# Two-head stores in 16 KB runs, and transposes on VectorE instead of TensorE, in a batched x·yᵀ kernel

## The chip, the cores and the metric

The kernel runs on one core of a Trainium2 chip. The time is the device time of one execution in microseconds. Ten runs of the kernel before have a median of 307.43 us (307.35 to 307.79).

## The reference

```python
batch, n_heads, seq_t, seq_s, channels = 8, 12, 512, 512, 64
def reference(x, y):        # x: [8, 12, 512, 64], y: [8, 12, 512, 64], float32
    return np.einsum('bhtc,bhsc->bhts', x, y).astype(np.float32)
```

There are 96 heads (batch and head together). Each multiplies a 512 x 64 matrix by the transpose of another one and gives a 512 x 512 matrix of float32. The inputs are 25.2 MB, the output is 100.7 MB. The contraction runs over 64 channels, which lie innermost in memory, while TensorE contracts over partitions: so channels must be brought onto partitions first.

## The kernel before

The heads are taken in 12 groups (`NG`) of 8. Within a group they stand as two sets `a` of four heads (`G = 4`). A head takes 32 partitions (`Q`), and a partition holds 16 consecutive rows (`R`) of it.

`load(g)` (L52) issues two DMAs of 1 MB from the SP queue, y and then x. In each, a partition receives two runs of 4 KB, one per set. Three groups are loaded ahead (`AHEAD`, the depth of `lpool`).

`prepare(g)` (L65) is a generator; each `yield` is a step that the main loop takes at a place of its choice. The first step casts y and x to bf16 on GpSimd (L73, four casts of 128 x 1024 elements) and issues the load for three groups later. Two steps transpose y: eight 128 x 128 transposes on TensorE against an identity matrix (L82) fill a PSUM tile `pt`, which is copied out by VectorE (L88) or ScalarE (L90). Two more do the same for x (L95, L100, L102). Channels are then on partitions, 64 for each of the two sets.

The main loop (L109) takes each group and each set `a`. An output tile `ot` has 128 partitions, each with 16 rows of 512 columns, 32 KB. For each pair of rows `k` it issues eight matmuls (L122): four heads, each with 32 columns of weights, into four 32-partition strips of `pm`, for two rows. ScalarE (L129) evicts even pairs from PSUM, VectorE (L131) odd ones. A step of the next group's `prepare` is taken at k = 0, 3 and 6 (L117). When the tile is full, one DMA of 4 MB stores it (L136): it is one contiguous piece of the output, a run of 32 KB per partition. The first and the last tile are stored in four pieces of 1 MB instead (L134).

All DMAs are issued on SP, in program order. A DMA that must wait holds back those behind it on SP. `ot` has three buffers: an eviction into a fourth tile waits until the first one's store has landed. Each engine takes its instructions in the order in which the scheduler of the framework wrote them.

Of the kernel before, what the change touches and what calls it, by code (L numbers as in the profile page):

```python
# [1 line left out]

# [5 lines left out]


@with_exitstack  # L10
def kernel(
    ctx: ExitStack,
    tc: tile.TileContext,
    x: bass.AP,
    y: bass.AP,
    out: bass.AP,
):

    nc = tc.nc
    B, H, T, C = x.shape
    _, _, S, _ = y.shape
    P = 128
    G = 4
    Q = P // G
    R = T // Q
    NG = B * H // (2 * G)  # L30
    K = R // 2
    AHEAD = 3
    fp32 = mybir.dt.float32
    bf16 = mybir.dt.bfloat16
    COPY = mybir.ActivationFunctionType.Copy
    assert C * 2 == P and S == T and R == 16

    xv = x.rearrange("b h t c -> (b h t c)").rearrange("(g a p n) -> g p a n", a=2, p=P, n=R * C)
    yv = y.rearrange("b h t c -> (b h t c)").rearrange("(g a p n) -> g p a n", a=2, p=P, n=R * C)
    ov = out.rearrange("b h t s -> (b h t s)").rearrange("(g a p n) -> g a p n", a=2, p=P, n=R * S)  # L40

    const = ctx.enter_context(tc.tile_pool(name="const", bufs=1))
    lpool = ctx.enter_context(tc.tile_pool(name="lpool", bufs=AHEAD))
    bpool = ctx.enter_context(tc.tile_pool(name="bpool", bufs=2))
    tpool = ctx.enter_context(tc.tile_pool(name="tpool", bufs=2))
    opool = ctx.enter_context(tc.tile_pool(name="opool", bufs=3))
    ptpool = ctx.enter_context(tc.tile_pool(name="ptpsum", bufs=2, space=bass.MemoryType.PSUM))
    pmpool = ctx.enter_context(tc.tile_pool(name="pmpsum", bufs=3, space=bass.MemoryType.PSUM))

    loaded = {}  # L50

    def load(g):  # L52
        xs = lpool.tile([P, 2, R, C], fp32)
        ys = lpool.tile([P, 2, R, C], fp32)
        nc.sync.dma_start(ys.rearrange("p a r c -> p a (r c)"), yv[g])  # L55
        nc.sync.dma_start(xs.rearrange("p a r c -> p a (r c)"), xv[g])
        loaded[g] = (xs, ys)

    for g in range(AHEAD):
        load(g)  # L60

    ident = const.tile([P, P], bf16)
    make_identity(nc, ident)

    def prepare(g, made):  # L65

        xs, ys = loaded.pop(g)
        yb = bpool.tile([P, R, 2, C], bf16)
        xb = bpool.tile([P, R, 2, C], bf16)
        for s, b in ((ys, yb), (xs, xb)):  # L70
            for half in range(2):
                rows = slice(half * K, (half + 1) * K)
                nc.gpsimd.tensor_copy(b[:, rows], s[:, :, rows].rearrange("p a r c -> p r a c"))  # L73
        if g + AHEAD < NG:
            load(g + AHEAD)
        yield
        yT = tpool.tile([P, G * Q, R], bf16)
        xT = tpool.tile([P, R, P], bf16)
        for half in range(2):
            pt = ptpool.tile([P, K, P], bf16)  # L80
            for k in range(K):
                nc.tensor.transpose(  # L82
                    pt[:, k, :], yb[:, half * K + k].rearrange("p a c -> p (a c)"), ident
                )
            dst = yT[:, :, half * K:(half + 1) * K]
            src = pt.rearrange("p k n -> p n k")
            if half == 0:
                nc.vector.tensor_copy(dst, src)  # L88
            else:
                nc.scalar.activation(dst, src, COPY)  # L90
            yield
        for half in range(2):
            pt = ptpool.tile([P, K, P], bf16)
            for k in range(K):
                nc.tensor.transpose(  # L95
                    pt[:, k, :], xb[:, half * K + k].rearrange("p a c -> p (a c)"), ident
                )
            dst = xT[:, half * K:(half + 1) * K]
            if half == 0:
                nc.vector.tensor_copy(dst, pt)  # L100
            else:
                nc.scalar.activation(dst, pt, COPY)  # L102
            yield
        made[g] = (xT, yT.rearrange("p n k -> p (n k)"))

    made = {}
    for _ in prepare(0, made):
        pass
    for g in range(NG):  # L109
        xT, yT = made.pop(g)  # L110
        steps = prepare(g + 1, made) if g + 1 < NG else iter(())
        for a in range(2):
            ot = opool.tile([P, R, S], fp32)
            otf = ot.rearrange("p r s -> p (r s)")
            edge = (g == 0 and a == 0) or (g == NG - 1 and a == 1)
            for k in range(K):
                if k in (0, 3, 6):  # L117
                    next(steps, None)
                pm = pmpool.tile([P, 2, S], fp32)
                for two in range(2):  # L120
                    for h in range(G):
                        nc.tensor.matmul(  # L122
                            pm[h * Q:(h + 1) * Q, two, :],
                            xT[a * C:(a + 1) * C, 2 * k + two, h * Q:(h + 1) * Q],
                            yT[a * C:(a + 1) * C, h * S:(h + 1) * S],
                            start=True, stop=True,
                        )
                if k % 2 == 0:
                    nc.scalar.activation(ot[:, 2 * k:2 * k + 2, :], pm, COPY)  # L129
                else:  # L130
                    nc.vector.tensor_copy(ot[:, 2 * k:2 * k + 2, :], pm)  # L131
                if edge and k % 2 == 1:
                    i, j = (2 * k - 2) * S, (2 * k + 2) * S
                    nc.sync.dma_start(ov[g, a][:, i:j], otf[:, i:j])  # L134
            if not edge:
                nc.sync.dma_start(ov[g, a], otf)  # L136


# [1 line left out]
_INS = ['x', 'y']  # L140
_OUTS = [((8, 12, 512, 512), 'float32')]


# [23 lines left out]
```

## Time and profile before

| | |
|---|---|
| profiled execution | 307.43 us |
| its span, first to last instruction | 305.7 us |
| instructions | 4378, of which PE 1920 matmuls and 1920 weight loads |
| busy share: PE, VectorE, ScalarE, GpSimd | 67%, 45%, 39%, 16% |
| HBM read, written | 25.17 MB, 100.66 MB, 412 GB/s over the span |
| granted PE clock | full to about 70 us, then half |
| 4 MB stores | 22, median 27.8 us from issue to landing |
| loads of 1 MB | 24, median 21.0 us (y) and 23.1 us (x) |

An idle engine costs nothing unless something waits for it. In a line of the costliest groups one reads: line, engine, operation, output and input with shapes, how often; then busy time in all and the mean of one in ns; then how long the engine stood idle before these instructions, and what ended most of that. In a line of the waits: engine, line and tile that waited, what ended the wait, us in all, how often, the longest. In a queue's line: kind, packets, MB, and the share of sixteen DMA engines' span that they took. A packet is one contiguous run that one DMA engine moves.

### The profile page before, as it was taken

The page shows a single profiled execution, that of the slowest core. Times are in us where ns is not written, and L with a number is a line of the kernel's source. Part 1 is how long each engine was busy: PE and PEld are TensorE (multiplying, and loading weights), DVE is VectorE, ACT ScalarE, POOL GpSimd, SP SyncE. Part 2 cuts the span into 40 slices and gives each one's busy share as a digit, 9 for nine tenths or more (in the row PEclk, how much of TensorE's full clock was granted, in tenths as well). Part 3 has the DMA queues.
Part 4 walks back from the last instruction along what each step waited for, and adds up shares of the span by engine and source line. Part 5 has one row for each costly group of instructions (what it writes and reads, how often), then busy time and mean ns, then how long its engine had stood idle before and what let it go on. Part 6 is the DMA issues. An engine that isn't in the chain of part 4 may idle for free.

```text
span 305.7 us, 4378 instructions
## 1 busy us (share of the span) xinstructions
PE 205.3 (67%) x1920; PEld 91.8 (30%) x1920; DVE 138.7 (45%) x120; ACT 119.7 (39%) x121; POOL 49.3 (16%) x54
## 2 busy tenths in 40 slices
PE   1899999969919918926953990980796976575000
PEld 1443234525304403512511530350252432222000
DVE  0465655657417607605633741670654664446000
ACT  1445537544423606605523441560644463325000
POOL 3754024300500500320140050041000000000000
PEclk9999999975555555755655555586555555555555
DMA  7999999999999999999999999999999999999980
GB/s 281 412 409 420 453 418 406 466 422 388 442 455 389 443 442 404 443 425 440 434 422 429 428 432 421 418 447 425 437 431 429 422 446 431 420 433 440 404 365 33
DMA packets 10867, 126.11 MB, mean 413 GB/s; under 512 B 864, under 2 KB 864, under 8 KB 7008
## 3 DMA queue, kind: packets, MB, share of 16 engines
q1 hardware_dynamic: 10848, 125.83, 97.2%
q8 instruction: 15, 0.25, 0.3%
q14 instruction: 4, 0.03, 0.0%
HBM read 25.17 MB, written 100.66 MB: 412 GB/s over the span
## 4 chain that ended last, share of the span: by engine, by line
DMA 49%; PE 30%; DVE 5%; issue 4%; ACT 3%; POOL 1%; SPq 0%; ACTq 0%
DMA out_dram<-ot 47%; PE pm L122 24%; DVE ot L131 4%; PE pt L95 4%; ACT ot L129 3%; DMA xs<-in_x_dram 2%; PE pt L82 2%; POOL xb L73 1%; ACT xT L102 0%; DVE xT L100 0%; SPq L55 0%; ACTq L129 0%; SPq L136 0%
## 5 line engine op out<-in xcount | busy, mean ns | idle before, releaser
L122 PE MATMUL pm<-yT,xT 64*32 64x512 bf16 x1536 | 160.7, 593 | 65.9 <-ACT ot L129 63.9
L131 DVE COPY ot<-pm 128x1024 f32<-128x1024 f32 x96 | 117.1, 1224 | 122.9 <-DMA out_dram<-ot 62.9
L129 ACT ACTIVATE ot<-pm 128x1024 f32<-128x1024 f32 x96 | 96.0, 1023 | 115.6 <-DMA out_dram<-ot 71.3
L122 PEld LDWEIGHTS <-xT 64*32 64x32 bf16 x1536 | 53.5, 119 | 147.9 <-issue 136.5
L73 POOL CAST yb<-ys 128x1024 bf16<-128x1024 f32 x24 | 24.3, 1041 | 143.6 <-PE pm L122 66.4
L82 PE MATMUL pt<-ident,yb 128*128 128x128 bf16 x192 | 24.2, 298 | 8.4 <-POOL yb L73 6.8
L102 ACT ACTIVATE xT<-pt 128x1024 bf16<-128x1024 bf16 x12 | 12.3, 1023 | 37.0 <-PE pt L95 30.2
L95 PE MATMUL pt<-ident,xb 128*128 128x128 bf16 x192 | 25.8, 310 | 1.3 <-DVE xT L100 0.8
L73 POOL CAST xb<-xs 128x1024 bf16<-128x1024 f32 x24 | 24.3, 1042 | 13.7 <-issue 4.9
L95 PEld LDWEIGHTS <-xb 128*128 128x128 bf16 x192 | 19.4, 143 | 22.6 <-issue 20.0
L82 PEld LDWEIGHTS <-yb 128*128 128x128 bf16 x192 | 19.5, 138 | 17.6 <-issue 8.2
L88 DVE COPY yT<-pt 128x1024 bf16<-128x1024 bf16 x12 | 14.6, 1215 | 8.4 <-PE pt L82 8.4
L90 ACT ACTIVATE yT<-pt 128x1024 bf16<-128x1024 bf16 x12 | 12.2, 1019 | 8.2 <-PE pt L82 8.2
L100 DVE COPY xT<-pt 128x1024 bf16<-128x1024 bf16 x12 | 8.3, 690 | 12.2 <-PE pt L95 9.7
L90 ACT ACT_TABLE_LOAD x1 | 1.3, 1283 | 0.7 <-PEq L151 0.7
masks.py:199 POOL TENSOR_SCALAR_AFFINE_SELECT ident<-ident 128x128 bf16<-128x128 bf16 x1 | 0.3, 292 | 0.1
masks.py:197 POOL MEMSET ident<- 128x128 bf16 x1 | 0.2, 204 | 0.3 <-POOLq L151 0.3
L151 POOL MEMSET const-float32-0.0<- 128x1 f32 x1 | 0.1, 98 | 0.2 <-issue 0.2
L151 POOL MEMSET const-bfloat16-1.0<- 128x1 bf16 x1 | 0.1, 102 | 0.0
L151 POOL MEMSET const-uint8-127<- 128x1 uint8 x1 | 0.1, 102 | 0.0
L151 POOL MEMSET const-float32-1.0<- 128x1 f32 x1 | 0.1, 98 | 0.0
## 6 DMA issues: line engine op xcount, KB each, us to landing
out_dram<-ot SPq DMA_DIRECT2D x22, 4096.0 KB, 27.8
ys<-in_y_dram SPq DMA_DIRECT2D x12, 1024.0 KB, 21.0
xs<-in_x_dram SPq DMA_DIRECT2D x12, 1024.0 KB, 23.1
out_dram<-ot SPq DMA_DIRECT2D x8, 1024.0 KB, 19.2
```

What stands on the lines that cost most here:

```text
L73: nc.gpsimd.tensor_copy(b[:, rows], s[:, :, rows].rearrange("p a r c -> p r a c"))
L82: nc.tensor.transpose(pt[:, k, :], yb[:, half * K + k].rearrange("p a c -> p (a c)"), ident)
L88: nc.vector.tensor_copy(dst, src)
L90: nc.scalar.activation(dst, src, COPY)
L95: nc.tensor.transpose(pt[:, k, :], xb[:, half * K + k].rearrange("p a c -> p (a c)"), ident)
L100: nc.vector.tensor_copy(dst, pt)
L102: nc.scalar.activation(dst, pt, COPY)
L122: nc.tensor.matmul(pm[h * Q:(h + 1) * Q, two, :], xT[a * C:(a + 1) * C, 2 * k + two, h * Q:(h + 1) * Q], yT[a * C:(a + 1) * C, h * S:(h + ...
L129: nc.scalar.activation(ot[:, 2 * k:2 * k + 2, :], pm, COPY)
L131: nc.vector.tensor_copy(ot[:, 2 * k:2 * k + 2, :], pm)
L151: nc = _bacc.Bacc("TRN2", target_bir_lowering=False, num_devices=1)
```

## The change

Groups are still 8 heads, but a head now takes 16 partitions (`G = 8`, `Q = 16`) of 32 rows each. A load puts one run of 8 KB on each partition. The four heads of a half group lie on 64 partitions.

`casts` casts in 32- and 64-partition pieces that also move data: the lower and the upper 32 channels of a half group go to different partitions of the bf16 tiles. For x, a pair of heads (`u`) has its own 32 partitions, and writes only its own slots of `xb`; the other slots are zeroed once at the start and stay zero. There are two such tiles, one per half.

`transposes` uses VectorE's transpose of 32 x 32 blocks, from SBUF to SBUF, for x and for y. The identity matrix, the transposes on TensorE and their PSUM tiles are gone, and `pm` has four buffers.

A matmul contracts over 128 partitions, channels of two heads, and its weights are 128 columns: 64 rows of head u = 0 interleaved with 64 of u = 1. The zeros in `xb` keep the two heads apart. One matmul thus serves two heads.

An output tile has 128 partitions of 8 rows, 16 KB, of two heads; neighbouring partitions belong to heads that are 2 MB apart in the output. Each tile is 2 MB and is stored whole. `ot` has seven buffers. VectorE evicts one pair of rows in four, ScalarE three. The order of all instructions is the order in which the program writes them (`manual_schedule`). For the first group the casts are shared among VectorE, ScalarE and GpSimd; later ones are all on GpSimd.

```diff
-    G = 4
+    G = 8
-    K = R // 2
+    K = 8
+    E = R // K
+    D = 32
-    ov = out.rearrange("b h t s -> (b h t s)").rearrange("(g a p n) -> g a p n", a=2, p=P, n=R * S)
+    ov = out.rearrange("b h t s -> (b h t s)").rearrange(
+        "(o u h q n) -> o h q u n", u=2, h=2, q=Q * E, n=K * S
+    )
...
+    zeroed = [const.tile([P, K, E, 2, D], bf16, name=f"xb{half}") for half in range(2)]
...
+    def casts(g, half, engines):
+        xs, ys = loaded[g]
+        xb = zeroed[half]
+        base = half * 64
+        n = 0
+        for ch in range(2):
+            for u in range(2):
+                lo = base + u * D
+                src = xs[lo:lo + D, :, ch * D:(ch + 1) * D]
+                cast(
+                    engines[n % len(engines)],
+                    xb[(2 * ch + u) * D:(2 * ch + u + 1) * D, :, :, u, :],
+                    src.rearrange("p (e k) c -> p k e c", k=K),
+                )
+                n += 1
+        yb = ybpool.tile([P, R, D], bf16)
+        for ch in range(2):
+            cast(
+                engines[n % len(engines)],
+                yb[ch * 64:(ch + 1) * 64],
+                ys[base:base + 64, :, ch * D:(ch + 1) * D],
+            )
+            n += 1
+        return xb, yb
+
+    def transposes(g, half, xb, yb):
+        xT = tpool.tile([P, K, 2, P], bf16)
+        nc.vector.transpose(
+            xT.rearrange("p k h m -> p (k h m)").rearrange("p (k r i) -> p k i r", k=K, i=2 * E),
+            xb.rearrange("p k e u c -> p k (e u) c"),
+        )
+        yT = tpool.tile([P, 2 * S], bf16)
+        nc.vector.transpose(yT.rearrange("p (r j) -> p j r", j=R), yb)
+        made[g, half] = (xT, yT)
+
+    def result(g, half, h, steps):
+        xT, yT = made[g, half]
+        ot = opool.tile([P, K, S], fp32)
+        for k in range(0, K, 2):
+            next(steps, None)
+            pm = pmpool.tile([P, 2, S], fp32)
+            for two in range(2):
+                nc.tensor.matmul(
+                    pm[:, two, :], xT[:, k + two, h, :], yT[:, h * S:(h + 1) * S], start=True, stop=True
+                )
+            if k == 4:
+                nc.vector.tensor_copy(ot[:, k:k + 2, :], pm)
+            else:
+                nc.scalar.activation(ot[:, k:k + 2, :], pm, COPY)
+        nc.sync.dma_start(ov[2 * g + half, h], ot.rearrange("p r s -> p (r s)"))
+
+    def prepare(g):
+        b = {}
+        for step in range(16):
+            if step in (0, 1):
+                b[step] = casts(g, step, [nc.gpsimd])
+            if step in (5, 13):
+                transposes(g, step // 8, *b[step // 8])
+            if step == 12 and g + AHEAD < NG:
+                load(g + AHEAD)
+            yield
+
+    with tc.manual_schedule():
+        for g in range(AHEAD):
+            load(g)
+        nc.vector.memset(zeroed[0], 0.0)
+        nc.gpsimd.memset(zeroed[1], 0.0)
+        b0 = casts(0, 0, [nc.vector, nc.scalar, nc.gpsimd])
+        transposes(0, 0, *b0)
+        b1 = casts(0, 1, [nc.gpsimd, nc.scalar])
+        transposes(0, 1, *b1)
+        if AHEAD < NG:
+            load(AHEAD)
+        for g in range(NG):
+            steps = prepare(g + 1) if g + 1 < NG else iter(())
+            for half in range(2):
+                for h in range(2):
+                    result(g, half, h, steps)
+            for _ in steps:
+                pass
```

## The prediction

> **What bounds the kernel now.** I read the slices first, then the windows at the end of the span, the queues, and the waits. Windows (columns: stretch, its length, busy time of each engine, granted PE clock, mean busy share of the 16 DMA engines, GB/s):
>
> ```profile
> 30.00:100.00 70.00, 59.35 (x553) 26.44 (x546) 38.43 (x35) 32.05 (x33) 12.16 (x12) 0.75 1.01 427
> 200.00:281.00 81.00, 57.40 (x552) 24.64 (x550) 41.51 (x35) 36.27 (x37) 4.05 (x4) 0.54 1.01 432
> 281.00:294.00 13.00, 0.00 (x0) 0.00 (x0) 1.22 (x1) 0.17 (x1) 0.00 (x0) 0.50 0.99 421
> 294.00:296.00 2.00, 0.00 (x0) 0.00 (x0) 0.00 (x0) 0.00 (x0) 0.00 (x0) 0.50 0.88 373
> 296.00:298.00 2.00, 0.00 (x0) 0.00 (x0) 0.00 (x0) 0.00 (x0) 0.00 (x0) 0.50 0.56 238
> 298.00:300.00 2.00, 0.00 (x0) 0.00 (x0) 0.00 (x0) 0.00 (x0) 0.00 (x0) 0.50 0.18 74
> 300.00:302.00 2.00, 0.00 (x0) 0.00 (x0) 0.00 (x0) 0.00 (x0) 0.00 (x0) 0.50 0.06 25
> 302.00:304.00 2.00, 0.00 (x0) 0.00 (x0) 0.00 (x0) 0.00 (x0) 0.00 (x0) 0.50 0.07 29
> ```
>
> Read two things. From 2 us to 294 us the DMA engines never rest. At the end they don't finish together: 0.06 is one engine of sixteen, alone for over 4 us. Completion records of the last store say the same: the first engine lands at 295.8, the fifteenth at 300.0, the last at 304.7; the span ends at 305.7. Every engine has the same bytes, so the end is set by one straggler, 8.9 us behind the leader.
>
> The waits, then the costliest groups and the queues, from the page:
>
> ```profile
> ACT ot L129 <- DMA out_dram<-ot: 71.3, 11, 9.4
> DVE ot L131 <- DMA out_dram<-ot: 62.9, 17, 8.8
> ```
> ```profile
> L131 DVE COPY ot<-pm 128x1024 f32<-128x1024 f32 x96 | 117.1, 1224 | 122.9 <-DMA out_dram<-ot 62.9
> L129 ACT ACTIVATE ot<-pm 128x1024 f32<-128x1024 f32 x96 | 96.0, 1023 | 115.6 <-DMA out_dram<-ot 71.3
> L73 POOL CAST yb<-ys 128x1024 bf16<-128x1024 f32 x24 | 24.3, 1041 | 143.6 <-PE pm L122 66.4
> L88 DVE COPY yT<-pt 128x1024 bf16<-128x1024 bf16 x12 | 14.6, 1215 | 8.4 <-PE pt L82 8.4
> ...
> q1 hardware_dynamic: 10848, 125.83, 97.2%
> q8 instruction: 15, 0.25, 0.3%
> ```
>
> Evictions wait for stores to free ot: compute is ahead, with three stores queued. What can move the time is the work of one DMA engine, the straggler, and any engine grown so slow that the queue runs dry.
>
> **Who makes the straggler.** The q8 row is 15 packets of 16 KB. In the trace each takes about 1.0 us, and each time one engine's data packet is also about 0.4 us long: that engine falls some 1.4 us back, a different one each time. The straggler shows something else: from 38 to 281 us nearly each of its 32 KB store packets lasts 40 to 100 ns over the usual 1213 ns, some 60, and none while instructions rest (184 to 190 us, or after 281). In all that is some 7 us. So the lag goes with instructions being run, 4378 of them.
>
> **What the Trainium skill says.** Four places of the Trainium skill bear on this. "Runtime: NRT & Kernel Launch", Instruction fetch mechanics: instructions are refilled in 16 KiB blocks, 256 instructions each. The trace agrees: PE's 3,848 instructions make 15.03 blocks, and 15 packets are there. "DMA: Bandwidth & Descriptors", Why a DMA increments its semaphore by 16: the engines used are the largest number up to 16 that divides the slowest dimension of both sides; 64 and 128 give 16. The trace before has only 128 on both sides. "GPSIMD Engine Reference", Engine selection: one-input operations run at roughly line rate; L73's 1041 ns for 1024 elements agrees. "Vector Engine (DVE) Microarchitecture Reference", 3.8: a 32x32 transpose sustains one element per cycle per lane. No VectorE transpose is in this trace; L88, unpacked copies at 1215 ns for 1024, is the nearest row.
>
> **The change, part by part.**
>
> *Bytes on one DMA engine.* Packet records of before, mean: 4 KB 162.4 ns, 8 KB 310.9, 32 KB 1217.7, completion 9. Before, each engine has 384 load packets (62.4 us), 64 stores of 8 KB (19.9), 176 of 32 KB (214.3) and 54 completions (0.5): 297.1 us. After: 192 loads of 8 KB (59.7), 384 stores of 16 KB and 72 completions (0.65). 16 KB isn't shown; between 8 and 32 KB the line gives 310.9 + 906.8/3 = 613 ns, so 235.4. Sum 295.8, or -1.3. With undisturbed packets (159, 309, 1213 ns, less 3 ns of overlap each) it is -0.5. I take -0.8. Lower bound of a 16 KB packet: half of 32 KB, 609 (-1.5 us more); upper: two of 8 KB, 622 (+3.5).
>
> *Instructions.* PE's transposes go (384 with their weight loads), and 1536 matmuls of 32 columns become 384 of 128 columns. By the two programs' instruction lists PE drops from 3,848 instructions to 776, 3.03 blocks; ACT rises from 167 to 241, VectorE 166 to 198, GpSimd 90 to 193, SP 116 to 153. All: 4,387 to 1,561, a factor 0.36. The steady 7.3 us of the straggler falls to 2.6; the block hits fall from 15 to 3. Lower bound of the lag after: one hit, 1.4 us. Upper: the lag of the second-worst engine before, 4.2. I take 2.8, so -6.1.
>
> *Engines, for a group of 8 heads. Its transfers take one DMA engine 16 x 310.9 + 32 x 613 ns = 24.6 us.* ACT: 12 evictions x 1023 = 12.3 us. VectorE: 4 x 1224 = 4.9, plus two transposes of 2048 and two of 1024 elements; at one element a cycle (L88's 1215 for 1024, so 2.3 for 2048) 7.0: 11.9 us. Lower bound, two elements a cycle as in L100's 690 ns for 1024: 8.9; upper, twice the price, since outputs lie 16 bytes apart: 18.9. GpSimd: 12 casts x 1.04 = 12.5 us, since 32 or 64 partitions save nothing along the row; lower bound the same, upper 2.0 each if the shift over partitions or the strided rows cost, 24. PE: 32 matmuls of 512 columns, at most L122's 593 ns each (its four column tiles overlap today; here there are none), 19.0 us. All lie beside the DMA's 24.6 and cost nothing; if that cover goes, every us over it counts 11 times.
>
> *Waits moved.* A cast waits for the transpose that last read xb; behind it on GpSimd are only the other casts. Transposes queue ahead of VectorE's eviction at two of four results: 3.5 us, for which that store waits on SP, and later stores behind it. With seven ot tiles some five stores of 4.9 us are queued; that hides it. load(3) and later loads wait on SP for casts: 24.6 us of slack.
>
> *Start.* The first six loads land every 2.56 us to 18.4, as before; load(3), issued once casts of group 0 end (about 12.6), lasts to 23.5. The first store: xs 5.6, ys 8.1; VectorE casts, then xT to 9.4, yT to 10.6, and the second pair behind ACT's and GpSimd's casts, 11.5 to 15.0; its eviction to 16.3. Issued at 16.4 and some 2 us to its first byte: 5 us before the queue is empty. Nothing. If the transposes cost double, the first two stores come some 3.5 us late in all. The last store is 2 MB instead of 1 MB, behind a backlog: nothing.
>
> *Sum.* The profiled execution took 307.43, its span 305.66, 1.77 around it; that is the median too. 307.43 - 0.8 - 6.1 = 300.5; 0.3 is added for the late start, 3.5 us at about one in twelve: 300.8.
>
> **Rivals.**
> 1. *The lag stays* (what slows the straggler isn't the number of instructions). For it: the excess is seen on one engine only, and its cause is inferred. Against: it stops when instructions stop. Then -0.8: 306.6, on the border of no change. 0.12.
> 2. *GpSimd becomes the bound*, slower than before. It has 144 casts instead of 48, of a shape that no row shows. It decides from 24.6/12 = 2.05 us a cast; at 2.5 times today's, 2.6 us, 31.2 a group: +73 us, 380. Against: today's strided casts run at one element per 1.02 ns. 0.06.
> 3. *The two-head store is slower per packet.* Its runs alternate between heads 2 MB apart, which no row shows. Each 1% is 2.35 us, so +3% (631 ns) eats the gain; at 5%, 312.6. 0.07.
> 4. *VectorE becomes the bound*: from 9.9 us a pair of transposes, against my 3.5. At four cycles an element 12.8: 30.5 a group, +65 us, 372. 0.03.
>
> **How the numbers follow.** Main case 0.72, its own range 299.2 (lag 1.4) to 304 (lag 4.2 and a late start). Rival 1 splits over faster and same. Faster by over 0.2% (under 306.8; 0.2% is about what a measurement tells from no change): 0.72 + 0.05 = 0.77. Same: 0.07. Slower: rivals 2 to 4, 0.16. Range 299.2 to 307.5: it takes in rival 1 and leaves out rivals 2 to 4 and the tails.
>
> **What would show it.** Right: DMA share 1.0 to about 294; the last store's 16 completions within 3 us; three q8 packets; 16 KB packets near 613 ns; evictions still wait for stores. Wrong: one engine at 0.06 for 4 us again (rival 1); ACT waiting for VectorE and that for GpSimd, DMA share under 1 (rivals 2, 4); longer store packets at share 1.0 (rival 3).

## The result, and the profile after

The kernel before took 307.43 us (median of 28 runs, 307.26 to 307.79), the changed kernel 449.09 us (8 runs, 448.98 to 449.21). The ratio is 1.4607, with a 95% interval of 1.4594 to 1.462. The forecast was 300.8 us, with a range of 299.2 to 307.5. It was wrong by 148 us, and on the wrong side.

First the page of the changed kernel: busy time, the slices of the span, and the queues.

```profile
PE 139.2 (31%) x377; PEld 49.6 (11%) x384; DVE 384.8 (86%) x99; ACT 144.5 (32%) x150; POOL 144.1 (32%) x142
...
DVE  5999999999889898898898988988989889889720
...
DMA  8904399597688498298298487668844826628497
...
q1 hardware_dynamic: 10368, 125.83, 68.3%
q8 instruction: 3, 0.05, 0.0%
```

The DMA engines had 97.2% of the span on the data queue before; now they have 68.3%. VectorE is at 9 or 8 in nearly every slice: the bound has moved there. Its costliest groups, and those of its neighbours:

```profile
L114 PE MATMUL pm<-yT,xT 128*128 128x512 bf16 x377 | 139.2, 540 | 290.0 <-DVE ot L118 266.0
L120 ACT ACTIVATE ot<-pm 128x1024 f32<-128x1024 f32 x144 | 137.9, 1030 | 280.9 <-PE pm L114 269.2
L98 DVE STREAM_TRANSPOSE xT<-xb 128x2048 bf16<-128x2048 bf16 x24 | 222.3, 9263 | 0.3 <-ACT xb L66 0.3
L68 POOL CAST xb<-xs 32x1024 bf16<-32x1024 f32 x91 | 94.5, 1039 | 232.3 <-DVE xT L98 225.7
L103 DVE STREAM_TRANSPOSE yT<-yb 128x1024 bf16<-128x1024 bf16 x24 | 116.0, 4833 | 0.0
L118 DVE COPY ot<-pm 128x1024 f32<-128x1024 f32 x48 | 62.9, 1317 | 40.1 <-issue 36.2
```

The transpose of x takes 9,263 ns, that of y 4,833. The forecast had 2.3 and 1.2 us. Together they are 338 of VectorE's 385 busy us. The two lengths give (9263 - 4833) / 1024 = 4.33 ns for each further element. Note the idle times too: GpSimd, ScalarE and PE stand idle for 232 to 290 us, all behind VectorE, ScalarE by way of PE.

The waits of the changed kernel tell that chain link by link (engine, line and tile that waits, what it waits for, us in all, times, longest):

```profile
ACT ot L120 <- PE pm L114: 269.2, 51, 11.5
PE pm L114 <- DVE ot L118: 266.0, 25, 12.6
POOL xb L68 <- DVE xT L98: 225.7, 22, 11.3
DVE ot L118 <- issue: 36.2, 18, 2.0
```

Before, the evictions waited for stores to free `ot`. Now ScalarE's eviction waits for PE, PE for VectorE's eviction to free `pm`, and GpSimd's cast for VectorE's transpose to free `xb`. No eviction waits for a store: the queue of stores is dry. A piece of the timeline, VectorE's with one line of PE's, shows one half group (start, length, instruction, the idle time before it in brackets):

```profile
207.19 9.27 DVE L98 STREAM_TRANSPOSE xT<-xb 128x2048 bf16<-128x2048 bf16 x1
216.09 4.83 DVE L103 STREAM_TRANSPOSE yT<-yb 128x1024 bf16<-128x1024 bf16 x1
220.57 1.40 DVE L118 COPY ot<-pm 128x1024 f32<-128x1024 f32 x1
222.03 6.49 PE L114 MATMUL pm<-yT,xT 128*128 128x512 bf16 x16 [12.60 <-DVE ot L118]
223.98 1.22 DVE L118 COPY ot<-pm 128x1024 f32<-128x1024 f32 x1 [2.01 <-issue]
225.13 9.26 DVE L98 STREAM_TRANSPOSE xT<-xb 128x2048 bf16<-128x2048 bf16 x1
```

From one transpose of x to the next it is 225.13 - 207.19 = 17.94 us. The eviction at 220.57 stood behind both transposes. PE had computed two more pairs of rows and then stopped; it starts again only when that eviction is done, after 12.60 us, and VectorE then idles for 2.01 us until PE has reached the result of its next eviction. A whole group takes 35.9 us where its transfers need 24.6. GpSimd does nothing during this transpose of x (it had been idle for 11.27 us when the transpose ended), so a clash of the two engines is not what makes it long.

That adds up to the time. The first store is issued at 36.6 us, behind the first two pairs of transposes; the third pair starts at 36.43. Four steps from pair to pair take 15.8 us each, without the idle time of 2.01 us, and the other 17 take 17.93. So the last pair starts at 404.45. The last store is issued 26.9 us later, at 431.3, and its last completion comes at 446.4; the span is 447.2.

### The profile page after: what moved, and what is told of

Read it like the earlier page. It is cut to its first block, busy times and chain, and to the rows that moved or that the text cites. A ratio compares the mean times of both kernels' runs of the same rounds, so it can differ in the third digit from the quotient of the medians.

```text
span 447.2 us, 1544 instructions
## 1 busy us (share of the span) xinstructions
PE 139.2 (31%) x377; PEld 49.6 (11%) x384; DVE 384.8 (86%) x99; ACT 144.5 (32%) x150; POOL 144.1 (32%) x142
## 3 DMA queue, kind: packets, MB, share of 16 engines
q1 hardware_dynamic: 10368, 125.83, 68.3%
## 5 line engine op out<-in xcount | busy, mean ns | idle before, releaser
L114 PE MATMUL pm<-yT,xT 128*128 128x512 bf16 x377 | 139.2, 540 | 290.0 <-DVE ot L118 266.0
L120 ACT ACTIVATE ot<-pm 128x1024 f32<-128x1024 f32 x144 | 137.9, 1030 | 280.9 <-PE pm L114 269.2
L98 DVE STREAM_TRANSPOSE xT<-xb 128x2048 bf16<-128x2048 bf16 x24 | 222.3, 9263 | 0.3 <-ACT xb L66 0.3
L68 POOL CAST xb<-xs 32x1024 bf16<-32x1024 f32 x91 | 94.5, 1039 | 232.3 <-DVE xT L98 225.7
L103 DVE STREAM_TRANSPOSE yT<-yb 128x1024 bf16<-128x1024 bf16 x24 | 116.0, 4833 | 0.0
L118 DVE COPY ot<-pm 128x1024 f32<-128x1024 f32 x48 | 62.9, 1317 | 40.1 <-issue 36.2
L114 PEld LDWEIGHTS <-xT 128*128 128x128 bf16 x384 | 49.6, 129 | 379.1 <-issue 350.9
L68 POOL CAST yb<-ys 64x1024 bf16<-64x1024 f32 x46 | 47.5, 1033 | 7.7 <-DVE yT L103 2.8
L68 DVE CAST xb<-xs 32x1024 bf16<-32x1024 f32 x2 | 2.1, 1058 | 3.9 <-DMA xs<-in_x_dram 3.8
L66 ACT ACTIVATE xb<-xs 32x1024 bf16<-32x1024 f32 x3 | 3.2, 1053 | 0.1
```

What stands on the lines that cost most here:

```text
L68: engine.tensor_copy(dst, src)
L98: nc.vector.transpose(xT.rearrange("p k h m -> p (k h m)").rearrange("p (k r i) -> p k i r", k=K, i=2 * E), xb.rearrange("p k e u c -> p k ...
L103: nc.vector.transpose(yT.rearrange("p (r j) -> p j r", j=R), yb)
L114: nc.tensor.matmul(pm[:, two, :], xT[:, k + two, h, :], yT[:, h * S:(h + 1) * S], start=True, stop=True)
L118: nc.vector.tensor_copy(ot[:, k:k + 2, :], pm)
L120: nc.scalar.activation(ot[:, k:k + 2, :], pm, COPY)
```

## The experiments

The first three questions are about the transposes, the others about the 300.8 us that were predicted with cheap ones. In every set of runs the kernel before had a median of 307.4 us, to within 0.1. e1_layouts and e5_layouts2 ran once each; only the lengths of their instructions are read.

**What an element of a transpose costs.** In e1_layouts each group of heads takes one of six forms of the two transposes, for instance:

```diff
+        if kind == 1:
+            nc.vector.transpose(xf, xs_)
+        if kind == 3:
+            nc.vector.transpose(
+                xf.bitcast(u32).rearrange("p (k r i) -> p k i r", k=K, i=E),
+                xs_.bitcast(u32).rearrange("p (k i c) -> p k i c", k=K, c=D),
+            )
```

> The changed kernel with its 24 pairs of VectorE transposes in six layouts, two groups of heads each; the output is not the product, since most layouts put the elements elsewhere. In layout 0 (as in the change: elements of 2 bytes, written 16 and 64 bytes apart) I expect 9.26 and 4.83 us. Theory A, the price is one of the transpose of 2-byte elements: about 4.33 ns an element in whatever order they are written, so contiguous (layout 1), 4 bytes apart (2) and 8 bytes apart (5) also take 9.3 and 4.8 us. Theory B, the price is that of the scattered writes: contiguous takes about 1 ns an element, 2.3 and 1.2 us, and the two other layouts lie between. For elements of 4 bytes, half as many (layouts 3 strided, 4 contiguous): 4.8 and 2.6 us if the price is per element, 9.3 and 4.8 if it is per byte, 1.2 and 0.7 if 4 bytes are one element per cycle.

The groups of that kernel. L105 and L108 are the forms of the change, L129 writes 8 bytes apart, L113 4 bytes apart, L110 without gaps; L118 and L126 are the same data as 4-byte elements, 16 bytes apart and without gaps.

```profile
L105 DVE STREAM_TRANSPOSE xT<-xb 128x2048 bf16<-128x2048 bf16 x4 | 37.2, 9308 | 0.3 <-ACT xb L67 0.3
L108 DVE STREAM_TRANSPOSE yT<-yb 128x1024 bf16<-128x1024 bf16 x4 | 19.4, 4840 | 0.0
L129 DVE STREAM_TRANSPOSE xT<-xb 128x2048 bf16<-128x2048 bf16 x4 | 18.9, 4724 | 0.0
L113 DVE STREAM_TRANSPOSE xT<-xb 128x2048 bf16<-128x2048 bf16 x4 | 9.9, 2467 | 0.0
L110 DVE STREAM_TRANSPOSE xT<-xb 128x2048 bf16<-128x2048 bf16 x4 | 9.2, 2297 | 0.0
L118 DVE STREAM_TRANSPOSE xT<-xb 128x1024 uint32<-128x1024 uint32 x4 | 8.3, 2075 | 0.0
L126 DVE STREAM_TRANSPOSE xT<-xb 128x1024 uint32<-128x1024 uint32 x4 | 4.9, 1235 | 0.0
```

Theory B holds: written without gaps, the same 2,048 elements take 2,297 ns, which is the figure that the forecast used. The price is in the distance between the elements written, and it goes up in steps: 2.3, 2.5, 4.7 and 9.3 us at 2, 4, 8 and 16 bytes. y, 64 bytes apart, pays hardly more per element than x at 16 (4.73 against 4.54 ns). A 4-byte element 16 bytes apart costs about 2.0 ns, less than half of a 2-byte one, and none of the three prices expected for it.

**Is it the transpose or the write?** e5_layouts2 has six more forms, made as in e1_layouts, among them plain copies with the same scattered writes:

```diff
+            nc.vector.tensor_copy(
+                xf.rearrange("p (k r i) -> p k i r", k=K, i=2 * E), xs_.rearrange("p (k i r) -> p k i r", k=K, i=2 * E)
+            )
```

> The changed kernel with six other layouts in the place of its transposes, two groups of heads each; the output is not the product, since the elements lie elsewhere. Lines in order: 2-byte transposes written 32 bytes apart; 2-byte transposes that read 16 and 64 bytes apart and write without gaps; 4-byte transposes written 8 bytes apart; plain bf16 copies (no transpose) written 16 and 64 bytes apart; plain copies without gaps; 4-byte transposes written 32 bytes apart. Theory B1, the scattered write is what costs, whatever the operation: reading apart costs nothing (2.3 and 1.2 us), the plain scattered copy costs as much as the scattered transpose (9.3 and 4.8 us). Theory B2, it is a matter of the transpose's write alone: reading apart costs nothing, the plain scattered copy costs no more than one element per cycle (2.3 and 1.2 us). Under both, 2-byte elements at 32 bytes cost no more than at 16 (9.3 and 4.8), 4-byte elements at 32 bytes as at 16 (2.1 and 1.0), and at 8 bytes between 1.2 and 2.1 us for 1024.

The groups of that kernel: L105 writes 2-byte elements 32 bytes apart, L110 reads 16 bytes apart and writes without gaps, L124 and L129 are plain copies, written 16 bytes apart and without gaps, L115 writes 4-byte elements 8 bytes apart.

```profile
L105 DVE STREAM_TRANSPOSE xT<-xb 128x2048 bf16<-128x2048 bf16 x4 | 35.5, 8868 | 0.3 <-ACT xb L67 0.3
L124 DVE COPY xT<-xb 128x2048 bf16<-128x2048 bf16 x4 | 19.7, 4937 | 0.0
L110 DVE STREAM_TRANSPOSE xT<-xb 128x2048 bf16<-128x2048 bf16 x4 | 15.4, 3849 | 0.0
L115 DVE STREAM_TRANSPOSE xT<-xb 128x1024 uint32<-128x1024 uint32 x4 | 5.0, 1239 | 0.0
...
L129 DVE COPY xT<-xb 128x2048 bf16<-128x2048 bf16 x4 | 3.2, 808 | 0.0
```

Neither theory holds whole. The plain scattered copy is slow as well, six times the plain copy without gaps (4,937 against 808 ns), so this is no matter of the transpose alone (B2 falls). Part of the factor of six is that the copy without gaps is fast: 0.39 ns an element, where the transpose without gaps took 1.12. But it is half as slow as the scattered transpose, so the two don't have one price (B1 falls as put). Reading apart isn't free either: 3,849 against 2,297 ns. As expected, 32 bytes cost no more than 16. 4-byte elements 8 bytes apart cost nothing extra.

**The transposes' work alone.** e4_act moves VectorE's evictions to ScalarE, so that nothing is queued behind the transposes.

```diff
-            if k == 4:
-                nc.vector.tensor_copy(ot[:, k:k + 2, :], pm)
-            else:
-                nc.scalar.activation(ot[:, k:k + 2, :], pm, COPY)
+            nc.scalar.activation(ot[:, k:k + 2, :], pm, COPY)
```

> The changed kernel with every eviction on ScalarE, so that VectorE has only the transposes. If VectorE's work with the wait in its queue is the bound: 2 x 14.1 = 28.2 us a group, 12 groups and about 20 us at start and end: 358 us, ScalarE at 16.5 us a group not the bound. If ScalarE or the matmuls set the time by now instead: no better than 449.

It took 353.68 us, near the 358 expected. From its page:

```profile
DVE  4999999999999999999999999999999999999900
...
L98 DVE STREAM_TRANSPOSE xT<-xb 128x2048 bf16<-128x2048 bf16 x24 | 231.2, 9634 | 0.3 <-ACT xb L66 0.3
```

VectorE is still the bound, with 48 transposes and no rest. So of the change's 449 us some 95 were not the transposes, but the four evictions per group and PE's standing still behind them: in the changed kernel VectorE was busy with evictions for 62.9 us and idle for 36.2 us before them.

**The rest of the change, with cheaper transposes.** e2_quarter transposes a quarter of the elements, with the writes as far apart as in the change:

```diff
+            xT.rearrange("p k h m -> p (k h m)").rearrange("p (k r i) -> p k i r", k=K, i=2 * E)[:, 0:2],
+            xb.rearrange("p k e u c -> p k (e u) c")[:, 0:2],
```

> The changed kernel with a quarter of the elements transposed (the rest of the transposed tiles stays zero, so three quarters of the contraction's inputs are left out); matmuls, evictions, casts, loads and stores are all there. The pair of transposes then takes some 4.3 us instead of 14.1. If the price of the transposes is all that failed in the prediction: VectorE needs about 14 us a group, the DMA engines set the time, 300.8 us with a lag of some 3 us at the end. If the lag of the last DMA engine does not follow the instructions: about 306.6, with one engine alone for over 4 us at the end. If GpSimd's casts or the two-head stores were also too slow: above 307, with casts over 2 us or 16 KB packets over 630 ns.

e3_pairs transposes all of them, but as pairs: the casts lay two bf16 numbers that end up side by side next to each other, and the transposes move them as one 4-byte element.

```diff
-                    xb[(2 * ch + u) * D:(2 * ch + u + 1) * D, :, :, u, :],
+                    xb[(2 * ch + u) * D:(2 * ch + u + 1) * D, :, :, :, u],
...
-            xT.rearrange("p k h m -> p (k h m)").rearrange("p (k r i) -> p k i r", k=K, i=2 * E),
-            xb.rearrange("p k e u c -> p k (e u) c"),
+            xT.rearrange("p k h m -> p (k h m)").bitcast(u32).rearrange("p (k r i) -> p k i r", k=K, i=E),
+            xb.rearrange("p k e c u -> p (k e c u)").bitcast(u32).rearrange("p (k e c) -> p k e c", k=K, e=E),
```

> The changed kernel with the transposes on pairs of bf16 numbers as one 4-byte element (pairs of u slots in x, pairs of rows in y, interleaved by the casts), so 1024 and 512 elements instead of 2048 and 1024. If the price is per element, 4.33 ns: 4.8 and 2.6 us, VectorE 20 us a group, under the 24.6 us of the DMA engines: about 301 us. If it is per byte: no change from the changed kernel, 449 us. GpSimd's casts then write 4 bytes apart: 1.04 us each as before if that costs nothing.

Both took the same: 304.97 and 304.98 us, ratios to the kernel before 0.9924 (0.9907 to 0.994) and 0.9923 (0.9908 to 0.9938). From the page, the waits and the windows of e3_pairs:

```profile
L69 POOL CAST xb<-xs 32x1024 bf16<-32x1024 f32 x91 | 120.3, 1323 | 49.6 <-DMA xs<-in_x_dram 32.4
L99 DVE STREAM_TRANSPOSE xT<-xb 128x1024 uint32<-128x1024 uint32 x24 | 49.4, 2060 | 12.8 <-POOL xb L69 11.0
L104 DVE STREAM_TRANSPOSE yT<-yb 128x512 uint32<-128x512 uint32 x24 | 24.9, 1038 | 5.7 <-POOL yb L69 5.6
```
```profile
DVE ot L122 <- DMA out_dram<-ot: 110.9, 33, 9.5
ACT ot L124 <- DMA out_dram<-ot: 102.6, 34, 7.9
```
```profile
100.00:200.00 100.00, 46.99 (x126) 15.80 (x128) 42.43 (x33) 45.83 (x49) 66.97 (x52) 0.67 1.01 427
20.00:22.00 2.00, 0.71 (x3) 0.19 (x2) 1.28 (x2) 2.00 (x3) 1.88 (x3) 1.00 0.90 291
22.00:24.00 2.00, 0.00 (x0) 0.00 (x0) 2.00 (x3) 0.22 (x1) 1.96 (x2) 1.00 0.97 360
296.00:298.00 2.00, 0.00 (x0) 0.00 (x0) 0.00 (x0) 0.00 (x0) 0.00 (x0) 0.50 0.39 164
298.00:300.00 2.00, 0.00 (x0) 0.00 (x0) 0.00 (x0) 0.00 (x0) 0.00 (x0) 0.50 0.21 90
300.00:302.00 2.00, 0.00 (x0) 0.00 (x0) 0.00 (x0) 0.00 (x0) 0.00 (x0) 0.50 0.12 49
```

The pair of transposes is down to 3.1 us, cheaper than at either price expected; evictions wait for stores again, and the DMA share is 1.01: the steady state is as the forecast had it. The casts pay for writing 4 bytes apart (1,323 against 1,039 ns), under cover. The change with a cheap transpose is thus faster than the kernel before by 2.4 us. But 304.97 in e2_quarter, where only the transposes were cut, misses the forecast by 4.2 us, which has to be found too. The last windows of e3_pairs show where: engines fall out one by one, with 3 and then 2 of 16 still busy. The last store's completions spread over 5.88 us in e3_pairs, against 8.88 before and 2.8 forecast.

**Is the lag due to instructions?** e6_extra adds 1,920 small memsets to the kernel before (the expectation says 1,760; the step runs for all 12 groups, 160 each):

```diff
+        for n in range(160):
+            nc.gpsimd.memset(idle[:, n % 4:n % 4 + 1], 0.0)
```

> The kernel before with 1,760 memsets of one column added on GpSimd, 160 a group, which nothing waits for; the computation is the same. If the last DMA engine's lag grows with the number of instructions run, of whatever engine (7.3 us for 4,378): about +3 us, 310.4, with the last of the 16 completions 11 to 13 us behind the first. If it goes with something else (the matrix engine's instructions, the DMAs' own packets): within 0.5 us of the kernel before, 307.4, with seven more instruction packets spread over other engines.

e7_split adds 2,304 instructions to PE in e3_pairs, with the same columns computed:

```diff
+                for c in range(0, S, 128):
+                    nc.tensor.matmul(
+                        pm[:, two, c:c + 128], xT[:, k + two, h, :], yT[:, h * S + c:h * S + c + 128],
+                        start=True, stop=True,
+                    )
```

> The kernel with pairs as 4-byte elements (e3_pairs), each matmul of 512 columns split into four of 128, each with its own weight load, so that TensorE has 3,080 instructions instead of 776; the computation is the same. If TensorE's instructions make the lag of the last DMA engine: nine more instruction packets, lag back to 8 to 9 us instead of 5.9, time 307 to 308 instead of 305.0. If not: 305.0 to 305.5, lag about 6. If the split matmuls make TensorE the bound: above 310 with the DMA share under 1.

e6_extra took 312.27 us (ratio 1.0158, 1.0143 to 1.0173), e7_split 307.19 (0.9996, 0.9988 to 1.0005), 2.2 us more than e3_pairs. Instruction packets, first of e6_extra, then of e7_split; before there were 15 on q8 and 4 on q14, in e3_pairs 3 and 6:

```profile
q8 instruction: 15, 0.25, 0.3%
q14 instruction: 19, 0.16, 0.1%
```
```profile
q8 instruction: 12, 0.20, 0.2%
q14 instruction: 6, 0.05, 0.0%
```

The prediction's rival 1 falls: instructions of either engine lengthen the time of a kernel whose DMA engines are not idle (their share is 1.01 from 30 to 281 us in both). Whether an instruction does it by being fetched or by what it does is not separated. In e6_extra the last store's completions spread over 11.36 us, and two engines, not one, are over 9 us behind; in e7_split, whose profiled run was the slowest of twelve (308.24 us), over 8.34. But e6_extra costs 4.8 us, not 3: the completions' mean came 2.3 us later too (300.3 against 298.0), and the first one 2.5 us (298.3 against 295.8), so the extra instructions slowed all engines somewhat.

**And due to nothing else?** Four kernels have the transfers alone, with the loads' and stores' shapes swapped in turn. The core of e9_dma:

```diff
+                    ot = ots[(4 * g + 2 * half + h) % 7]
+                    nc.sync.dma_start(ov[2 * g + half, h], ot.rearrange("p r s -> p (r s)"))
+                    if half == 1 and h == 0 and g + AHEAD + 1 < NG:
+                        load(g + AHEAD + 1)
```

The four expectations are those of e9_dma, e10_dma_before, e11_loads4 and e12_loads8, in this order.

> The transfers of the changed kernel alone (loads of 1 MB in 8 KB packets, stores of 2 MB in 16 KB packets, in about its order); all of the computation is left out, the stores send zeros, and some 90 instructions are left. If the lag of the last DMA engine comes with instructions run beside the transfers: the last of the 16 completions within 1.5 us of the first, undisturbed packets (309 and 611 ns) make 294.6 us, and the time is about 299.5. If the lag comes from these transfers themselves: last completion some 5 us behind, 304.

> The transfers of the kernel before alone (loads in 4 KB packets, stores of 4 MB in 32 KB packets, the first and last in four parts); all of the computation is left out, the stores send zeros. If the lag comes with instructions: last completion within 1.5 us of the first, undisturbed packets (159, 309 and 1213 ns) make 294.8 us, and the time is about 299.5, the same as with the transfers of the changed kernel. If the transfers themselves make it: last completion some 8 us behind, 307.

> The transfers of the changed kernel alone as in e9_dma (303.9 us, last completion 3.6 us behind), but with loads in 4 KB packets as in the kernel before; all of the computation is left out, the stores send zeros. In e9_dma the lag grows only while loads pass, up to 223 us. If the 8 KB loads make it: as with the transfers of before, lag under 1 us, 300.5. If the two-head stores of 16 KB packets, or the loads passing between them, make it: lag 3 to 4 us, 303 to 304.

> The transfers of the kernel before alone as in e10_dma_before (300.5 us, last completion 0.7 us behind), but with loads in 8 KB packets as in the changed kernel; all of the computation is left out, the stores send zeros. If the 8 KB loads make the lag of e9_dma: 303 to 304, lag 3 to 4 us. If the two-head stores make it: 300.5, lag under 1 us.

A fifth has the stores of e11_loads4 laid out in one run each:

```diff
-    ov = out.rearrange("b h t s -> (b h t s)").rearrange(
-        "(o u h q n) -> o h q u n", u=2, h=2, q=Q * E, n=K * S
-    )
+    ov = out.rearrange("b h t s -> (b h t s)").rearrange("(o h p n) -> o h p n", h=2, p=P, n=K * S)
```

> The transfers of e11_loads4 (loads in 4 KB packets, stores of 2 MB in 16 KB packets, 302.7 us, last completion 3.7 us behind), but each store writes 2 MB without a gap instead of runs that alternate between two heads; all of the computation is left out, the stores send zeros. If the alternation between heads makes the lag: under 1 us, 300 to 300.5. If it is the size of the stores or of their packets: lag 3 to 4 us, 302.7.

| transfers alone | loads | stores | us, median | lowest, highest of 4 | profiled run | its last completion behind first |
|---|---|---|---|---|---|---|
| e10_dma_before | 4 KB | 4 MB, 32 KB | 300.51 | 299.60, 301.79 | 299.60 | 0.67 |
| e12_loads8 | 8 KB | 4 MB, 32 KB | 299.97 | 299.46, 300.34 | 299.67 | 1.06 |
| e9_dma | 8 KB | 2 MB, 16 KB, two heads | 303.92 | 302.65, 304.22 | 302.65 | 3.60 |
| e11_loads4 | 4 KB | 2 MB, 16 KB, two heads | 302.69 | 301.54, 302.92 | 302.92 | 3.72 |
| e13_onerun | 4 KB | 2 MB, 16 KB, one run | 302.62 | 301.37, 302.87 | 302.56 | 3.23 |

The windows at the end, first of e10_dma_before, then of e9_dma (two engines appear in them, since nothing runs on the others):

```profile
294.00:296.00 2.00, 0.00 (x0) 0.00 (x0) 1.00 0.99 418
296.00:298.00 2.00, 0.00 (x0) 0.00 (x0) 1.00 0.05 21
298.00:300.00 2.00, 0.00 (x0) 0.00 (x0) 1.00 0.00 0
```
```profile
294.00:296.00 2.00, 0.00 (x0) 0.00 (x0) 1.00 0.99 426
296.00:298.00 2.00, 0.00 (x0) 0.00 (x0) 1.00 0.42 180
298.00:300.00 2.00, 0.00 (x0) 0.00 (x0) 1.00 0.19 82
```

This splits the matter. With the transfers of before and no computation, the 16 engines end together in the profiled run: nearly all of that kernel's lag came with what is run beside them. By the medians that is 307.4 - 300.5 = 6.9 us, by the slowest and the fastest run of the transfers alone 5.6 to 7.8. With the transfers of the change they lag without any computation. Neither the loads' packet size (e11_loads4, e12_loads8) nor the alternation between heads (e13_onerun) makes this lag, though 8 KB loads may cost something besides: the median of e9_dma is 1.2 us above that of e11_loads4, with ranges that overlap. What is left is that the stores come as 48 of 2 MB in 16 KB packets in place of 22 of 4 MB and 8 of 1 MB. Which of size, number and order does it stays open.

In e9_dma the lag grows only while loads pass, not up to 223 us as the expectation of e11_loads4 has it: the store that lands at 214 us has all of it, and the last load packet starts at 216.7. It is load packets that are long there: 323 ns on the mean against a median of 309, while the stores' 16 KB packets took 611. But the 8 KB packets of e12_loads8 have a mean of 317 and its engines end together, so long load packets alone don't make the lag; how they fall on the engines isn't shown.

In the traces with computation, store packets and load packets can be told apart too. Store packets of 16 or 32 KB that lasted 20 to 150 ns over the usual 611 or 1213 ns, the mark of the straggler in the prediction, number 116 in the kernel before (7.3 us on all engines together) and 3 in e10_dma_before (0.1 us); 149 in e6_extra (9.0 us); 34 in e3_pairs (1.1 us) and 152 in e7_split (6.1 us). So this part of the lag goes with instructions, as predicted. What is left of it in e3_pairs comes while loads pass: the completions of the store that lands at 212 us are already spread over 5.9 us, those of the last one over 5.88, though the last eviction and the last store's issue come only at about 271 us.

**A thin queue at the start.** e8_ahead4 changes two sizes of e3_pairs:

```diff
-    AHEAD = 3
+    AHEAD = 4
-    opool = ctx.enter_context(tc.tile_pool(name="opool", bufs=7))
+    opool = ctx.enter_context(tc.tile_pool(name="opool", bufs=6))
```

> The kernel with pairs as 4-byte elements (e3_pairs), with loads four groups ahead instead of three and six ot tiles instead of seven. In e3_pairs the first store is issued at 24.0 us and the queue runs thin: 291 and 360 GB/s in the stretches 20 to 22 and 22 to 24 us against 430, about 1 us lost. With a fourth pair of loads in the queue at the start that is covered: 304.0. If the thin queue is not what slows the packets there: 305.0. If six ot tiles are too few: slower.

It took 304.02 us, ratio 0.9889 (0.9874 to 0.9903), the fastest of the versions that compute the whole product. Its windows at the start:

```profile
20.00:22.00 2.00, 0.63 (x3) 0.19 (x2) 1.29 (x2) 2.00 (x3) 1.88 (x3) 1.00 1.00 418
22.00:24.00 2.00, 0.01 (x1) 0.01 (x1) 2.00 (x3) 0.15 (x1) 1.96 (x2) 1.00 1.03 430
```

The dip is filled, and the time is the one expected. The reason isn't shown, though: the mean of the last store's completions came only 0.2 us earlier (297.9 against 298.1), while the last one came 1.2 us nearer to that mean. With the same 1,544 instructions, the lag fell from 5.88 to 4.71. And the dip doesn't come from a late first store: in the trace of e3_pairs the first store is issued at 16.7 us, and it is the second that comes at 24.0; and the dip is there in e9_dma (356 and 373 GB/s) and e12_loads8 (299 and 340), whose first stores were issued by 9.4 us. By 100 us e3_pairs and e8_ahead4 had moved the same 41.1 MB. So the expected time was met for a reason that isn't known.

## Why the prediction was wrong

*What bounds the kernel now*, right. The transfers of before alone need 300.5 us at the median, and the other 6.9 us come with the computation beside them.

*VectorE's work for a group*: this is the step that failed, and it decided the result. It priced the transposes "at one element a cycle" and gave "twice the price, since outputs lie 16 bytes apart" as the upper end. Measured: 4.5 ns an element, 4.0 times the same transpose without gaps. The figure quoted from the Trainium skill, "Vector Engine (DVE) Microarchitecture Reference", 3.8, agrees with what was measured without gaps, 2,297 ns for 2,048 elements; the step took it for a scattered output. Another page of the Trainium skill bears on that, "SBUF — State Buffer", Door 1: SBUF has 16-byte lines, an access that crosses into a new line pays, and two hits a line are needed for full bandwidth. It gives no price. The runs fit it in part: beyond 16 bytes the price didn't rise (8,868 ns at 32 bytes), and at 8 bytes, two to a line, 4-byte elements went at full rate. But 2-byte elements, also two to a line there, cost double (4,724 ns), and a step of 8 bf16, which the page calls free, is the one that cost four times. There the measurement decides. That these lines are the cause was not tested. The diff shows the distance in the output pattern (`i=2 * E`, eight elements of 2 bytes).

*Waits moved*, wrong as a consequence. The two transposes were to hold up VectorE's eviction for 3.5 us, covered by queued stores. They took 14.1, with no store queued, and PE stopped behind the eviction: 449.1 against 353.7 us once the evictions were taken out of that queue.

*Rival 4* named the mechanism and its threshold (9.9 us a pair), but gave it 0.03 and 372 us. It added 11 times 5.9 us. A group took 35.9 us instead of 30.5: its 12.8 us a pair is less than four times the step's own 3.5, which is 14.0, and it left out the wait behind the evictions. It also left out the start, where the first store comes at 36.6 us and not at 16.4.

*Instructions*, right in the mechanism, and near in size partly by luck. The transfers of the change alone take 303.9 us and e3_pairs 305.0: what the computation adds fell from 6.9 to 1.1 us, so by 5.8 where 6.1 was forecast. Three instruction packets were forecast and found. The medians behind this rest on four runs each, which lie up to 2.2 us apart. The long store packets fell from 7.3 to 1.1 us in all, where the step had 7.3 to 2.6 for the straggler. But the lag isn't all of instructions: it is 4.71 to 5.88 us with 1,544 of them, 2.8 having been forecast, so it fell by 3.0 to 4.2 us.

*Bytes on one DMA engine*, right on the stores' packets, wrong on the loads' and wrong as a measure. 16 KB packets had a mean of 611.8 ns in e3_pairs, for 613 (632 in the changed kernel, with a median of 615). But the 310.9 ns of an 8 KB packet came from stores, since the loads of before have 4 KB; 8 KB load packets had a mean of 320.7 in e3_pairs. With these two figures the step's sum is 297.2 us, not 295.8, and the gain over 297.1 is gone. Besides, it counts packets alone, and the engines don't share delays evenly: the change's transfers alone take 303.9 - 300.5 = 3.4 us more. Rival 3 had put such a loss on slower store packets; those were as fast as forecast.

So without the price of the transposes: 307.4 - 5.8 + 3.4 = 305.0, which only puts the measured times in the forecast's terms; the forecast had 307.4 - 6.1 - 0.8 + 0.3 = 300.8. It would have been faster than before and inside the whole range, but outside the main case's own, which ended at 304.

*Start*, right once the transposes are cheap: the first store is issued at 16.7 us in e3_pairs, for 16.4. *GpSimd*, right: 1.04 us a cast. *ScalarE and PE*, right: 1,030 ns an eviction, matmuls at 540 ns against at most 593, and both had time to spare.

## What to carry to other kernels

Before giving a rearrangement to VectorE, work out how many bytes lie between neighbouring elements of its output, and price it by that: a rate for dense data can be four times too good for 2-byte elements that land 16 bytes apart, and pairing them into 4-byte elements in an earlier pass made the same job cost 3.1 us instead of 14.1. A cheap operation hidden beside others is safe only within its margin; when the upper end of its price is a guess, look at what is queued behind it on its engine, because that costs extra (95 us here). Where DMA bounds, the time is that of the last of 16 engines, and a kernel with the transfers alone shows how much of that comes from the transfers and how much from the work beside them.

## What was not expected of the hardware

- Transposes on VectorE: 2,297, 2,467, 4,724 and 9,308 ns for 2,048 elements of 2 bytes written 2, 4, 8 and 16 bytes apart; 1,235, 1,239 and 2,075 ns for 1,024 elements of 4 bytes at 4, 8 and 16 bytes.
- A plain bf16 copy written 16 bytes apart took 4,937 ns instead of 808. A transpose that reads 16 bytes apart took 3,849 instead of 2,297.
- 1,920 memsets of one column on a GpSimd that was busy for 16% of the span cost a DMA-bound kernel 4.8 us, with 15 more packets of 8 KB on the second instruction queue.
- Store packets 20 to 150 ns over the usual length: 116 in the kernel before, with 4,378 instructions, and 3 with its transfers alone.
- The same bytes in 48 stores of 2 MB instead of 22 of 4 MB and 8 of 1 MB, with nothing else running, spread the ends of the 16 DMA engines over 3.2 to 3.7 us instead of 0.7 to 1.1 (five profiled runs, one of each kernel).
